# Moving tiles in SBUF so that no 256-column precise product of a two-model chain has both operands at one offset mod 256

## The chip, the cores and the metric

The kernel runs on one core of a Trainium2 chip. The metric is the device time of one execution in microseconds (us). The chip's TensorE (PE) does the matrix products, VectorE (DVE) and ScalarE (ACT) the elementwise work, GpSimd (POOL) a little of it, and SyncE (SP) issues most of the DMA.

## The reference

Two small transformers are chained: `first_block` gives x, `second_block` goes on with it. All arithmetic is float32, with 256 tokens and a width of 1024. The second model is what most of the time goes to:

```python
def second_block(x, positions, norm1_g, w_in, ..., w_up, w_down, final_g):
    for l in range(DEPTH):                      # 2 layers
        h = rmsnorm(x, norm1_g[l])
        z = h @ w_in[l]                         # 4 mixers' inputs and 4*1024 gate columns
        o_mla = mla_mixer(...); o_nsa = nsa_mixer(...)
        o_fox = fox_mixer(...); o_dsa = dsa_mixer(...)
        branches = jnp.stack([o_mla, o_nsa, o_fox, o_dsa], axis=2)
        lifted = jnp.einsum('bsnc,ncd->bsnd', branches, w_branch[l])
        gates = jax.nn.sigmoid(z_gate.reshape(B, S, N_BRANCH, D_MODEL))
        x = x + jnp.sum(gates * lifted, axis=2) @ w_out[l]
        h2 = rmsnorm(x, norm2_g[l])
        x = x + jnp.square(jax.nn.relu(h2 @ w_up[l])) @ w_down[l]   # 1024 -> 4096 -> 1024
    return rmsnorm(x, final_g)
```

`first_block` has two layers too: an even mixer (attention and pooling) and an odd mixer (gating and convolution), each followed by a mixture of experts with 16 experts, two for each token.

## The kernel before, in words

**Precise products.** TensorE multiplies in float32r, and one product of that is not precise enough. So `split` (L139 to L141) makes two tiles of each operand: ACT copies the value to a float32r tile (hi), DVE subtracts that from the value (lo). `mm3` (L167 to L170) then issues three products for one: hi by hi, hi by lo, lo by hi. Each has a stationary tile of 128x128 weights (`whi` or `wlo`), loaded by a LDWEIGHTS that the profile shows as PEld, and a moving tile of 128 partitions x 256 tokens of the activations. Such a product is called a 256-column product below, and a run of them over one half of a weight chunk a stream: 8 weight tiles, 24 products. `token_linear` (L201 to L203) has it the other way round: activations stand, 512 columns of weights move.

**Staging.** A chunk of weights is a 1 MB DMA into a slot of `ring` or `ring_b` (`chunk`, L132 on). `half` (L146 on) splits each half of it into `whi` and `wlo` of a staging pool, two buffers each, and turns to the next pool of the list `stages` for the next half. That list is `[stage]` in the first model, `[stage, stage_b]` in the second model, and `[stage, stage_b, ml]` in its feed-forward, where the pool `ml` is appended (L1638). So neighbouring streams read their weights from different pools.

**Pools.** Pools are laid out one behind the other in SBUF: `const`, `ring`, `stage`, then for the first model `c1` and `ring_b`, or for the second `wk`, `stage_b`, and behind them `at0`/`at1` (attention) or `ml0`/`ml1` (feed-forward). A change of a small tile in `const` shifts everything behind it. A tile's offset mod 256 below is its byte address within a partition modulo 256, as the built program has it; each 128-column weight tile takes 512 bytes and each 256-column moving tile 1024, so all products of a stream have the same two offsets. Before the change these are:

| stream (moving tile) | its offset | weights from: their offset |
|---|---|---|
| gates and other products with the normed x (`act`) | 0 | stage 0, stage_b 64 |
| branch lift `lf` and feed-forward up `fm` (`oT`) | 0 | stage 0, stage_b 64, ml 192 |
| output `fm` of the mixed branches (`mx`) | 64 | stage 0, stage_b 64 |
| feed-forward down `d` (`hid`) | 64 | stage 0, stage_b 64, ml 192 |
| mixers' `ah`/`al` of the first model | 0 | stage 0 |
| odd mixer's `mix` | 32 | stage 0 |

The **difference** of a stream is its weights' offset less its moving tile's, mod 256. It is 0 for 3175 pairs of neighbours among the program's 256-column products, 64 for 1650, 128 for 526, 192 for 1175, others for 656.

**Order of the work.** In attention `fill` (L1221 on) puts gate streams between the steps of the mixers, so that TensorE has work while softmax and top-k run on the other engines; the order is fixed in the program. The feed-forward of a layer (`up` at L1642, `down` at L1653) alternates up and down: 16 chunks each, each of two streams. The compressed attention makes `dv` (a doubled copy of the values, by POOL, L1411), transposes it on TensorE (`vct`, L1412), copies that on ACT (`vcT`, L1414), adds positions on POOL (`cblk`, L1426) and multiplies it with weights on TensorE (`cmp`, L1433 for keys, L1436 for values).

## Time and profile before

| | |
|---|---|
| runs | 1494.27, 1494.14, 1490.57 us; median 1494.14 us |
| profiled execution, own time | 1494.22 us |
| its span (first to last instruction) | 1492.5 us |
| mean granted TensorE clock | 0.985 of full speed |
| PE busy | 1453.1 us, 97% |
| DVE, ACT busy | 57%, 44% |
| DMA | 324.85 MB, mean 218 GB/s |

The span is one execution on the chip. An engine's share tells how much of the span it had an instruction running; matmuls overlap, so the busy time of a group of them (its count by its mean duration) is more than the time it takes, and the time that one product costs is the distance from its start to the next one's start.

### The profile page before, as it was taken

How to read it: one execution, taken by the hardware profiler on the slowest of the kernel's cores; microseconds unless marked ns; L12 is line 12 of the kernel's file. 1: busy time of each engine (PE TensorE's matmuls, PEld its weight loads, DVE VectorE, ACT ScalarE, POOL GpSimd, SP SyncE). 2: the span in 40 equal slices, each digit the busy share in tenths (PEclk: the TensorE clock that was granted, in tenths of full speed). 3: DMA queues.
4: the chain of work that ended last, by engine and by line, in shares of the span. 5: the costliest groups of instructions: out<-in, count | busy, mean ns of one | idle time of the engine just before them, and what ended most of it. 6: DMA issues, size and time to landing. Idle time of an engine off the chain costs nothing.

```text
span 1492.5 us, 25477 instructions
## 1 busy us (share of the span) xinstructions
PE 1453.1 (97%) x10370; PEld 1168.0 (78%) x10372; DVE 851.7 (57%) x1666; ACT 654.1 (44%) x1108; POOL 27.3 (2%) x63
## 2 busy tenths in 40 slices
PE   8999899989999998999999999999999999999998
PEld 3756644446985443798789999999898799999998
DVE  2765452126637222758776765556759767755554
ACT  2544311124433111565664554444565654644443
POOL 0000000000000000010000000000100000000000
PEclk9999999999999999999999999999999999999999
DMA  9964799949484986644125555553443234555540
GB/s 394 400 283 171 296 372 366 398 167 374 173 335 191 404 360 238 211 158 171 58 90 193 191 205 183 185 197 143 155 167 144 69 131 170 188 208 198 177 162 29
DMA packets 47006, 324.85 MB, mean 218 GB/s; under 512 B 5601, under 2 KB 5985, under 8 KB 8481
## 3 DMA queue, kind: packets, MB, share of 16 engines
q1 hardware_dynamic: 45360, 320.12, 56.3%
q8 instruction: 86, 1.41, 0.4%
q10 hardware_dynamic: 1296, 1.55, 0.3%
q0 software_dynamic: 224, 1.46, 0.3%
q14 instruction: 40, 0.32, 0.1%
HBM read 322.06 MB, written 1.05 MB: 216 GB/s over the span
## 4 chain that ended last, share of the span: by engine, by line
PE 57%; DVE 2%; ACT 1%; issue 0%; DVEq 0%; ACTq 0%
PE fm L169 10%; PE fm L170 10%; PE fm L168 10%; PE d L169 4%; PE d L168 4%; PE d L170 4%; PE sp L1504 1%; PE tm L201 1%; PE tm L202 1%; PE tm L203 1%; PE lf L169 1%; PE lf L170 1%; PE lf L168 1%; PE po L1493 1%; PE ptp L1487 1%; DVE wlo L141 1%
## 5 line engine op out<-in xcount | busy, mean ns | idle before, releaser
L141 DVE TENSOR_TENSOR wlo<-w,whi 128x1024 fp32r<-128x1024 f32 (+1 forms) x314 | 378.4, 1208 | 254.1 <-ACT whi L140 252.9
L140 ACT CAST whi<-w 128x1024 fp32r<-128x1024 f32 (+1 forms) x314 | 324.3, 1035 | 388.2 <-PE fm L169 234.7
L168 PE MATMUL fm<-acth,whi 128*128 128x256 f32 x592 | 169.4, 286 | 0.0
L169 PE MATMUL fm<-actl,whi 128*128 128x256 f32 x592 | 168.2, 284 | 0.0
L170 PE MATMUL fm<-acth,wlo 128*128 128x256 f32 x592 | 167.9, 284 | 0.0
L170 PE MATMUL d<-hidh,wlo 128*128 128x256 f32 x512 | 144.1, 282 | 0.0
L169 PE MATMUL d<-hidl,whi 128*128 128x256 f32 x512 | 144.0, 281 | 0.0
L168 PE MATMUL d<-hidh,whi 128*128 128x256 f32 x512 | 143.9, 281 | 0.0
L169 PE MATMUL fm<-oTl,whi 128*128 128x256 f32 x512 | 143.6, 281 | 0.0
L170 PE MATMUL fm<-oTh,wlo 128*128 128x256 f32 x512 | 143.3, 280 | 0.0
L168 PE MATMUL fm<-oTh,whi 128*128 128x256 f32 x512 | 143.1, 280 | 0.0
L169 PEld LDWEIGHTS fm<-actl,whi 128*128 128x128 f32 x592 | 112.5, 190 | 2.3 <-issue 2.3
L168 PEld LDWEIGHTS fm<-acth,whi 128*128 128x128 f32 x592 | 113.1, 191 | 1.0 <-issue 0.8
L170 PEld LDWEIGHTS fm<-acth,wlo 128*128 128x128 f32 x592 | 112.4, 190 | 1.3 <-issue 1.0
L169 PEld LDWEIGHTS fm<-oTl,whi 128*128 128x128 f32 x512 | 96.8, 189 | 0.4 <-DVE oTl L1118 0.4
L169 PEld LDWEIGHTS d<-hidl,whi 128*128 128x128 f32 x512 | 96.7, 189 | 0.4 <-DVE hidl L141 0.4
L168 PEld LDWEIGHTS fm<-oTh,whi 128*128 128x128 f32 x512 | 96.9, 190 | 0.0
L168 PEld LDWEIGHTS d<-hidh,whi 128*128 128x128 f32 x512 | 96.8, 189 | 0.1
L170 PEld LDWEIGHTS d<-hidh,wlo 128*128 128x128 f32 x512 | 96.8, 189 | 0.1
L170 PEld LDWEIGHTS fm<-oTh,wlo 128*128 128x128 f32 x512 | 96.8, 189 | 0.0
L600 PE MATMUL yp<-w,ht 128*64 128x512 f32 (+1 forms) x272 | 71.8, 622 | 6.6 <-PEq L791 3.2
L566 PE MATMUL gu<-w,ug 128*64 128x512 f32 x256 | 62.2, 598 | 0.0
(537 smaller groups left out, 2875.1 us busy)
## 6 DMA issues: line engine op xcount, KB each, us to landing
w<-gu SPq DMA_DIRECT2D x64, 1024.0 KB, 8.7
w<-mod SPq DMA_DIRECT2D x48, 1024.0 KB, 10.7
w<-dn SPq DMA_DIRECT2D x32, 1024.0 KB, 10.0
w<-gw SPq DMA_DIRECT2D x32, 1024.0 KB, 4.8
w<-up SPq DMA_DIRECT2D x32, 1024.0 KB, 4.7
w<-dw SPq DMA_DIRECT2D x32, 1024.0 KB, 4.7
w<-tm SPq DMA_DIRECT2D x12, 1024.0 KB, 4.9
w<-oin SPq DMA_DIRECT2D x8, 1024.0 KB, 8.8
```

The costliest lines, as they stand in the source:

```text
L140: A.copy(hi, src)
L141: V.tensor_sub(lo, src, hi.bitcast(F32))
L168: T.matmul(out, ws[0], xs[0], start=first, stop=False, skip_group_check=skip)
L169: T.matmul(out, ws[0], xs[1], start=False, stop=False, skip_group_check=skip)
L170: T.matmul(out, ws[1], xs[0], start=False, stop=last, skip_group_check=skip)
L201: T.matmul(ps, at[0], ww[0], start=first, stop=False, skip_group_check=True)
L202: T.matmul(ps, at[1], ww[0], start=False, stop=False, skip_group_check=True)
L203: T.matmul(ps, at[0], ww[1], start=False, stop=k == NK - 1, skip_group_check=True)
L566: T.matmul(gu[each * e:each * e + each, :], x_[:, 4 * h + k, s0 + CAP * e:s0 + CAP * e + each], w[e][:, 512 * k:512 * k + 512], start=(h = ...
L600: T.matmul(yp[each * e:each * e + each, :], ht[:, 128 * k + each * e:128 * k + each * e + each], wd[e][:, 1024 * k + 512 * q:1024 * k + 51 ...
L1487: T.transpose(tp[:, 128 * c:128 * c + 128], prs[g][:, 128 * c:128 * c + 128], ident)
L1493: T.matmul(po[64 * g:64 * g + 64, 0:S], vals(g, 0), prs[g][:, 0:S], start=first, stop=False, tile_position=(0, 64 * g), skip_group_check=True)
```

## The change: what it does, and the diff

The diff has three kinds of edits. A new function `apart` puts a tile of n floats at the beginning of a pool, which a memset on DVE fills once: 16 floats in `c1` and in `wk`, 48 in `at0`, `at1`, `ml0` and `ml1`. The gap within `ml` grows from 32 to 48 floats. And tiles are made smaller or shared: `epst` 8 floats instead of 16, one `g2` for both layers, `vss` in an existing tile, and `m8` (the eight maxima of top-k) and `dv` with one buffer instead of two.

`epst` and `g2` take 64 bytes from `const`, so that `ring` and `stage` begin at 192 instead of 0 mod 256; the 16 floats of `c1` and `wk` put back what lies behind them. The 48 floats move what lies in `at` and in `ml` ahead of the gap by 192.

```diff
+        def apart(pool, n):
+
+            V.memset(pool.tile([128, n], F32, name=f"gap{n}", tag=f"gap{n}"), 0.0)
...
         ring_b = b1.enter_context(tc.tile_pool(name="ring_b", bufs=7))
+        apart(c1, 16)
...
-        epst = const.tile([128, 16], F32, name="epst")[:, 0:1]
+        epst = const.tile([128, 8], F32, name="epst")[:, 0:1]
...
-            g2 = const.tile([128, NK], F32, name=f"g2_{layer}")
+            g2 = const.tile([128, NK], F32, name="g2", tag="g2")
...
-            ss = wk.tile([128, 8], F32, name="vss")
+            ss = wk.tile([128, S], F32, name="vss", tag="dg")[:, 0:8]
...
         wk = es.enter_context(tc.tile_pool(name="b2", bufs=1))
+        E["apart"](wk, 16)
...
             at = ph.enter_context(tc.tile_pool(name=f"at{l}", bufs=1))
+            E["apart"](at, 48)
...
-                    m8 = at.tile([128, 8], F32, name="m8", tag="m8", bufs=2)
+                    m8 = at.tile([128, 8], F32, name="m8", tag="m8")
...
-                dv = at.tile([128, 2, 64], F32, name="dv", tag="dv", bufs=2)
+                dv = at.tile([128, 2, 64], F32, name="dv", tag="dv")
...
             ml = ph.enter_context(tc.tile_pool(name=f"ml{l}", bufs=1))
+            E["apart"](ml, 48)
...
-                    V.memset(ml.tile([128, 32], F32, name="gap", tag="gap"), 0.0)
+                    V.memset(ml.tile([128, 48], F32, name="gap", tag="gap"), 0.0)
```

Offsets mod 256 in the program built from it: `ring` and `stage` 192, `stage_b` 64, `ml`'s weights 192; `act`, `oT`, `ah`/`al`, `mx`, `hid`, `mix` all 0. So a stream's difference is now that of its pool alone: 192 from `stage` and from `ml`, 64 from `stage_b`. In pairs of neighbours: 0 for 204 (in the experts' scatter, where no split weights take part), 64 for 2420, 192 for 4074, others for 466.

The products are the same, in the same number. Two places are in another order. With one buffer of `dv`, its second copy on POOL must follow the first transpose, and TensorE's second transpose stands behind half of the keys' `cmp` products. TensorE in layer 1 before:

```order
L1412 MATMUL vct<-cst,dv 128x128 [waits Activation_49]
L1412 MATMUL vct<-cst,dv 128x128
L1433 MATMUL cmp<-cblk,w 64x16 [waits DMAHW3_49,Activation_49,Pool_49]
L1433 MATMUL cmp<-cblk,w 64x16 x7
L1433 MATMUL cmp<-cblk,w 64x16 [waits Pool_49]
L1433 MATMUL cmp<-cblk,w 64x16 x7
L1504 MATMUL sp<-fk,fq 128x128 x2
```

and now:

```order
L1419 MATMUL vct<-cst,dv 128x128 [waits Activation_49]
L1440 MATMUL cmp<-cblk,w 64x16 [waits DMAHW3_49,Activation_49,Pool_49]
L1440 MATMUL cmp<-cblk,w 64x16 x7
L1419 MATMUL vct<-cst,dv 128x128 [waits Pool_49]
L1440 MATMUL cmp<-cblk,w 64x16 x8
L1511 MATMUL sp<-fk,fq 128x128 x2
```

`vct` is the tile of transposed values, `cmp` the compressed keys, `sp` the next scores. The second transpose waits for POOL (its copy of `dv`) and stands behind 8 of the 16 `cmp` products; on POOL the second copy went behind the four sums of `cblk` for the keys and waits for TensorE. The second layer has the same.

The memsets of the gaps come where their pools first open. DVE at the end of the first model and the start of the second before (`ygl` and `y` are the last experts' outputs, `xT` the residual sum, `actl` the lo part of the second model's first activations):

```order
L606 SCALAR_TENSOR_TENSOR ygl<-yp,cws,ygh 128x512 [waits Activation_49]
L425 SCALAR_TENSOR_TENSOR xT<-y_4537,g_1_4541,xT 128x256 [waits PE_49]
L141 TENSOR_TENSOR wlo<-w,whi 128x1024 [waits DMAHW4_49,DMAHW3_49,DMAHW5_49,DMAHW2_49,DMAHW6_49,DMAHW1_49,DMAHW7_49,DMAHW0_49,Activation_49]
L606 SCALAR_TENSOR_TENSOR ygl<-yp,cws,ygh 128x512 [waits Activation_49]
L1118 SCALAR_TENSOR_TENSOR actl<-xT,pf,acth 128x256 [waits Activation_49]
L425 SCALAR_TENSOR_TENSOR xT<-y_4537,g_1_4541,xT 128x256
L141 TENSOR_TENSOR wlo<-w,whi 128x1024 [waits Activation_49]
L1118 SCALAR_TENSOR_TENSOR actl<-xT,pf,acth 128x256 [waits Activation_49]
L425 SCALAR_TENSOR_TENSOR xT<-y_4538,g_1_4541,xT 128x256 [waits PE_49]
L425 SCALAR_TENSOR_TENSOR xT<-y_4538,g_1_4541,xT 128x256
```

and now:

```order
L80 MEMSET gap_6265 128x16 [waits DMAHW3_49,DMAHW2_49,DMAHW4_49,DMAHW1_49,DMAHW5_49,DMAHW0_49,DMAHW6_49,DVE_49,DMAHW7_49,PE_49,Activation_49]
L611 SCALAR_TENSOR_TENSOR ygl<-yp,cws,ygh 128x512 [waits Activation_49]
L430 SCALAR_TENSOR_TENSOR xT<-y_4539,g_4543,xT 128x256 [waits PE_49]
L146 TENSOR_TENSOR wlo<-w,whi 128x1024 [waits DMAHW2_49,Activation_49]
L611 SCALAR_TENSOR_TENSOR ygl<-yp,cws,ygh 128x512 [waits Activation_49]
L1124 SCALAR_TENSOR_TENSOR actl<-xT,pf,acth 128x256 [waits Activation_49]
L430 SCALAR_TENSOR_TENSOR xT<-y_4539,g_4543,xT 128x256
L146 TENSOR_TENSOR wlo<-w,whi 128x1024 [waits Activation_49]
L80 MEMSET gap_6279 128x48 [waits DMASW1_49,DMASW2_49,DMASW0_49,DMASW3_49,SP_sequencer_49,DMASW4_49,DVE_sequencer_49,DMASW5_49,PE_sequencer_49,DMASW6_49,Activation_sequencer_49,DMASW7_49,Pool_sequencer_49,DMAHW6_49,DVE_49,PE_49]
L1124 SCALAR_TENSOR_TENSOR actl<-xT,pf,acth 128x256 [waits Activation_49]
L430 SCALAR_TENSOR_TENSOR xT<-y_4540,g_4543,xT 128x256 x2
```

The gap of `wk` stands ahead of the residual sums and waits for the first model's last readers of that memory, the gap of `at0` stands between the second model's first `actl` tiles and waits for TensorE's last product of the experts; the two sums behind it no longer have that wait of their own. On DVE, too, each MAX of top-k now follows the MATCH_REPLACE that reads the one `m8`. The gap of `at1` stands the same way at the start of the second layer. The order on SP is the same.

## Rows read from the trace of the kernel before

**Rows 1.** The page, part 1: busy time, share, instructions of each engine.

```profile
PE 1453.1 (97%) x10370; PEld 1168.0 (78%) x10372; DVE 851.7 (57%) x1666; ACT 654.1 (44%) x1108; POOL 27.3 (2%) x63
```

**Rows 2.** Windows: stretch; busy us by engine; PEclk; DMA share; GB/s.

```profile
470.00:605.00 135.00, 128.97 (x657) 60.41 (x656) 48.01 (x135) 29.99 (x50) 1.23 (x6) 0.99 0.84 335
...
700.00:770.00 70.00, 69.51 (x522) 55.25 (x520) 50.35 (x153) 44.89 (x133) 0.00 (x0) 0.99 0.26 92
...
870.00:1055.00 185.00, 185.00 (x1517) 182.47 (x1516) 107.22 (x121) 88.04 (x108) 0.96 (x5) 1.00 0.50 177
```

**Rows 3.** Instructions by line, PE: group xcount | busy us, mean ns.

```profile
L168 PE MATMUL fm<-acth,whi 128*128 128x256 f32 x592 | 169.4, 286 | 0.0
...
L168 PE MATMUL d<-hidh,whi 128*128 128x256 f32 x512 | 143.9, 281 | 0.0
...
L168 PE MATMUL fm<-oTh,whi 128*128 128x256 f32 x512 | 143.1, 280 | 0.0
...
L168 PE MATMUL fm<-ah,whi 128*128 128x256 f32 x192 | 54.9, 286 | 0.3 <-DVE mod L406 0.3
```

**Rows 4.** Timeline, PE, feed-forward: start us, duration us of each stream's first product.

```profile
910.50 0.28 PE L168 MATMUL fm<-oTh,whi 128*128 128x256 f32 x1
...
927.61 0.28 PE L168 MATMUL d<-hidh,whi 128*128 128x256 f32 x1
...
930.46 0.28 PE L168 MATMUL d<-hidh,whi 128*128 128x256 f32 x1
...
933.29 0.29 PE L168 MATMUL fm<-oTh,whi 128*128 128x256 f32 x1
...
936.02 0.28 PE L168 MATMUL fm<-oTh,whi 128*128 128x256 f32 x1
...
938.74 0.28 PE L168 MATMUL d<-hidh,whi 128*128 128x256 f32 x1
...
941.46 0.28 PE L168 MATMUL d<-hidh,whi 128*128 128x256 f32 x1
...
944.34 0.28 PE L168 MATMUL fm<-oTh,whi 128*128 128x256 f32 x1
```

**Rows 5.** Timeline, PE, gate streams in attention: first products of three streams.

```profile
783.25 0.28 PE L168 MATMUL fm<-acth,whi 128*128 128x256 f32 x1
...
786.07 0.28 PE L168 MATMUL fm<-acth,whi 128*128 128x256 f32 x1
...
788.95 0.28 PE L168 MATMUL fm<-acth,whi 128*128 128x256 f32 x1
```

**Rows 6.** Timeline, PE, odd mixer: the first and last of 313 products.

```profile
374.03 0.28 PE L170 MATMUL fm<-ah,wlo 128*128 128x256 f32 x1
...
411.47 0.28 PE L170 MATMUL fm<-ah,wlo 128*128 128x256 f32 x1
```

**Rows 7.** Timeline, PE, ACT and POOL around the value transposes of layer 1.

```profile
694.71 0.38 PE L1412 MATMUL vct<-cst,dv 128*128 128x128 f32 x2
...
695.02 2.04 PE L1433 MATMUL cmp<-cblk,w 128*64 128x16 f32 x32
...
696.18 1.79 POOL L1426 TENSOR_TENSOR cblk<-vcT,pe 64x120 f32<-64x120 f32 x4 [34.44 <-ACT vcT L1414]
...
698.55 1.25 PE L1436 MATMUL cmp<-w,cblk 128*16 128x64 f32 x10
```

**Rows 8.** Timeline, DVE, ACT, PE where the second model begins.

```profile
599.55 0.87 DVE L425 SCALAR_TENSOR_TENSOR xT<-y,g,xT 128x256 f32<-128x256 f32 x2
...
600.86 0.91 ACT L1117 ACTIVATE acth<-xT,pf 128x256 fp32r<-128x256 f32 x2
...
601.41 0.73 PE L201 MATMUL tm<-whi,acth 128*128 128x512 f32 x2 [0.52 <-ACT acth L1117]
```

**Rows 9.** DMA issues: KB of one, median us from issue to landing.

```profile
pw<-pool_w SPq DMA_DIRECT2D x1, 256.0 KB, 2.6
sgw<-sg_w ACTq DMA_DIRECT2D x1, 256.0 KB, 4.2
```

## The prediction, made before the changed kernel ran

> **What bounds the kernel now.** I read the page's shares first, then windows by stage, then the groups of products by line, and last the timeline of TensorE alone, where the time of a product is the distance between starts. The shares say that PE is busy for 97% of the span [rows 1]; the reader is to see that no other engine comes near. The windows say where it has no slack at all: in the feed-forward of layer 1 PE is busy for 185.00 us of 185.00, with DMA at half its share and the clock at 1.00; in attention for 69.51 of 70 [rows 2]. So almost all of the second model is as long as its products, and what a product costs decides. The groups by line say which they are: 592, 512, 512 and 192 products on each of the three lines of `mm3` [rows 3].
>
> Their mean durations differ a little, 286 against 280 ns, though they are the same work. The timeline tells what this goes with. In the feed-forward each stream of 24 products has one pair of offsets, and in the order of rows 4 the differences are: from 927.61 `hid` with ml, 128; from 930.46 `hid` with stage, 192; from 933.29 `oT` with stage_b, 64; from 936.02 `oT` with ml, 192; from 938.74 `hid` with stage, 192; from 941.46 `hid` with stage_b, 0. A stream's length by 24 gives the spacing [rows 4]:
> - difference 128: 2.85 us, 118.8 ns
> - 192 at 930.46: 2.83 us, 117.9 ns
> - 64, 192 and 192 after it: 2.73, 2.72 and 2.72 us, 113.3 to 113.8 ns
> - 0: 2.88 us, 120.0 ns
>
> The gate streams in attention alternate: at 783.25 with stage_b, difference 64, 2.82 us or 117.5 ns; at 786.07 with stage, difference 0, 2.88 us or 120.0 ns [rows 5]. In the odd mixer, where all weights come from stage at difference 0, 312 spacings take 37.44 us, 120.0 ns each [rows 6]. So a difference of 0 always costs 120.0, and others have two levels, about 117.7 and 113.4. A stream behind one at 0 or 128 has the slower one here; once a stream is at the faster one, the next non-zero stream stays there.
>
> **What the change does to the products.** No stream keeps a difference of 0 or 128; each has 64 or 192. What they cost then no row shows for long. The nearest stretch is the one from 930.46 to 941.46, four streams with neither 0 nor 128: 11.00 us for 96 products, 114.6 ns [rows 4]. It is bounded below by 113.4, every stream at the faster level, and above by 117.7, every stream at the slower one. I take 115.5, half of the products at either level: nearer to the stretch than to the upper end, but with returns to the slower level allowed for, since in that stretch the moving tile also changes between `hid` at 64 and `oT` at 0, which it no longer does.
> - **Feed-forward.** 512 up and 512 down products on each of three lines [rows 3], 3072. A cycle of twelve streams from 910.50 to 944.34 takes 33.84 us for 288 products, 117.5 ns [rows 4]. 3072 x (117.5 - 115.5) = 6.1 us gained.
> - **Gates and the rest with `act`.** 592 x 3 = 1776 [rows 3]. Half at 120.0, half at 117.5 [rows 5], mean 118.8. 1776 x 3.3 = 5.9 us.
> - **Branch lift.** 8 chunks of 16 weight tiles, three products each, 384 by the code, with the offsets of the gates: 384 x 3.3 = 1.3 us. The products of the mixed branches are as many, with one class at 0 and one at 192, as in the feed-forward: 384 x 2.0 = 0.8 us.
> - **Odd mixer and the even one's output.** 192 x 3 = 576 [rows 3], from 120.0 [rows 6]. They have one pool, so a run of one difference; I take the slower level, which a stream has that starts behind something else: 576 x 2.3 = 1.3 us.
> - The `mix` products had a difference other than 0 before, and the 512-column ones of `token_linear` move other tiles; for both I count nothing.
>
> Sum: 6.1 + 5.9 + 1.3 + 0.8 + 1.3 = 15.4 us gained.
>
> **What it costs.** The transposes. Before, both run at 694.71, `cmp` follows at 695.02 for 2.04 us, POOL starts `cblk` for the values at 696.18 once `vcT` is there, and PE waits 0.63 us at 698.55 for POOL's last sum [rows 7]. Now the second transpose is behind half of `cmp`, 1.0 us later. ACT's copy, then POOL's sums and the values' `cmp` are late by what isn't covered, with nothing on PE's queue able to pass. Between 0 and 1.0 us a layer. I take 0.3: POOL started only at 696.18, 1.1 us after the transposes ended, so ACT's copy between them was late for another reason and covers most of it. For two layers 0.6. POOL's second copy itself waits for the first transpose and is short beside the 1.0 us.
>
> The memset of `at0`'s gap stands, with its chain of semaphores, ahead of the residual sums that start at 599.55 and take 0.87, until 600.42; ACT begins the activations from them at 600.86, and PE waits 0.52 us for those at 601.41 [rows 8]. 0.44 us of DVE's delay are covered there, the rest is PE's. The wait itself takes the place of the one that the two sums behind it had for the same products. Between 0 and 0.6 us; I take 0.2. The gap of `at1` waits for PE where a sum waited for PE before; the others are in idle stretches of DVE, which is busy for 107.22 us of 185 [rows 2]. MAX behind MATCH_REPLACE costs nothing, as each already reads what the other wrote.
>
> Cover. In attention, products shortened beside a chain on DVE and ACT give back only where PE would not wait instead. PE idles 0.49 us of 70 [rows 2], so most of the gain stays; I take off 0.7 us, 200 gate products of either layer at half of 3.3 ns.
>
> 15.4 - 0.6 - 0.2 - 0.7 = 13.9 us. From the profiled execution's 1494.22 us, 0.08 over the median of the runs, this gives 1480.3, so **1480 us**.
>
> **Rivals.**
> - **The faster level holds throughout.** Nothing in rows 4 ends it but a difference of 0, and none is left. At 113.4: feed-forward 12.6, gates 9.6, lift 2.1, mixed branches 1.6, mixers 3.8, together 29.7; less 1.5 of costs, 28.2: 1466 us. Against it: streams at 64 and 192 sit at the slower level too, for all their 24 products [rows 4, 5], with no drift back.
> - **The difference does little.** Every stream settles at 117.7, the level of those that start behind another kind of work. Then the feed-forward loses 0.6 us, gates gain 2.0, lift 0.4, the mixed branches nothing and mixers 1.3; less 1.5 it is 1.6 us: 1492.6. It includes that the offsets only go along with something else, such as which engine writes at the time; against that, `hid` with stage is fast and `hid` with stage_b is slow within 3 us [rows 4]. The Trainium skill, page "TensorE: Matmul & The Clock Gate", section "Part 2: What happens when you issue a matmul", speaks for no effect: PE has two independent read ports into SBUF, and "Loading the next tile's weights doesn't steal SBUF read bandwidth from the running matmul", by which no offset could matter and the time would be 1494.2 plus the 0.8 us of costs, 1495. The trace does not agree: 2.88 against 2.72 us for the same 24 products [rows 4].
> - **Slower: the ring's slots are no longer aligned.** Four of the slots that 1 MB weight loads go to now begin at 192 mod 256. `sgw`, which began at 32 mod 256, took 4.2 us for 256 KB, `pw` at offset 0 took 2.6 [rows 9], a factor of 1.6, with other traffic beside both. The experts of the second layer load at a DMA share of 0.84 [rows 2]; with 4 of 13 turns of the list `rings` there through `ring`, a factor f makes that 0.84 x (1 + 4/13 x (f - 1)). It decides from f = 1.6, where the share is 1.0. At f = 2 it is 1.10: 135 us become 148, and if the first layer's experts lose half as much, 20 us are lost against 14 won, 1500 us. Against it: the ratio of rows 9 holds one transfer each, issued from different queues at different times.
>
> **Chances.** The middle forecast (1471 to 1488) 0.53, the faster level throughout 0.26, little effect 0.16, slower through loads 0.05. The range has to reach to the faster level and leaves out the last two: 1465 to 1490, 0.79. A measurement of this kernel tells some 0.3% or 4.5 us from no change: faster is below 1489.7, slower above 1498.6. Faster: 0.53 + 0.26 + 0.02 of the little effect = 0.81. Same: 0.14. Slower: 0.05.
>
> **What would show it.** In the changed kernel's timeline of the feed-forward, a cycle of twelve streams should take 33.3 us instead of 33.84 (32.7 if the faster level holds, 33.9 if the slower), with no stream of 2.88 or 2.85. In attention no gate stream should take 2.88. In the odd mixer 312 spacings should take 36.7 us. The PE wait ahead of the values' `cmp` should grow from 0.63 to about 0.9, and the wait at the second model's start from 0.52 to about 0.7. The windows of the experts (470 to 605) should keep their length; if they grow with DMA near 1.00, the loads are slower. The prediction is wrong if streams without a difference of 0 still take 2.88 us, or if DVE or a load becomes what PE waits for in the feed-forward.

## The result, and the profile after

The changed kernel takes 1474.95 us, the median of four runs from 1471.55 to 1478.32, against 1494.12 before; the ratio is 0.9882 with a 95% interval from 0.9859 to 0.9906. The prediction was 1480 us within 1465 to 1490. Run again beside two experiments it took 1476.28 us, ratio 0.9891 [0.9874, 0.9909]. The kernel before took a median of 1491.25 to 1491.94 us beside the experiments, 2 to 3 us less than beside this first result, so by medians the gain is 15.6 to 19.2 us. The profiled execution is the longest of the first four, 1478.32 us with a span of 1476.5, so the two traces differ by 16.0 us of span, less than the medians do.

The page of the changed kernel, parts 1 and 5 (two groups as in rows 3, now on L173 and L175):

```profile
PE 1435.1 (97%) x10370; PEld 1148.0 (78%) x10372; DVE 852.4 (58%) x1672; ACT 654.3 (44%) x1108; POOL 27.3 (2%) x63
...
L173 PE MATMUL fm<-acth,whi 128*128 128x256 f32 x592 | 166.7, 282 | 0.0
...
L175 PE MATMUL fm<-acth,wlo 128*128 128x256 f32 x592 | 165.0, 279 | 0.7 <-DVE wlo L146 0.7
```

PE is busy for 97% of the span as before [rows 1] and does the same 10370 instructions in 18 us less. The gates' mean duration fell from 286 to 282 ns [rows 3]. What a product costs is again read from starts. TensorE's timeline in the feed-forward of layer 1, first products of every fourth stream and of a cycle's end:

```profile
884.40 0.28 PE L173 MATMUL fm<-oTh,whi 128*128 128x256 f32 x1
...
895.71 0.28 PE L173 MATMUL fm<-oTh,whi 128*128 128x256 f32 x1
...
906.59 0.28 PE L173 MATMUL fm<-oTh,whi 128*128 128x256 f32 x1
...
939.23 0.28 PE L173 MATMUL fm<-oTh,whi 128*128 128x256 f32 x1
```

From 884.40 to 895.71 four streams (96 products) take 11.31 us, 117.8 ns a product: the slower level. The four from 895.71 to 906.59 take 10.88, 113.3 ns, and from 906.59 to 939.23 the cycle of twelve streams takes 32.64 us where before it took 33.84 [rows 4]. No stream falls back from there to the layer's last product, at 1031.6. In attention, the gate streams from stage_b and from stage (rows 5 before):

```profile
777.07 0.28 PE L173 MATMUL fm<-acth,whi 128*128 128x256 f32 x1
...
779.79 0.28 PE L173 MATMUL fm<-acth,whi 128*128 128x256 f32 x1
...
782.51 0.28 PE L173 MATMUL fm<-acth,whi 128*128 128x256 f32 x1
```

Both take 2.72 us, 113.3 ns. In the odd mixer, with one pool, the first and last of 319 products (rows 6 before):

```profile
373.20 0.28 PE L175 MATMUL fm<-ah,wlo 128*128 128x256 f32 x1
...
410.65 0.28 PE L175 MATMUL fm<-ah,wlo 128*128 128x256 f32 x1
```

37.45 us for 318 spacings, 117.8 ns: the slower level all through. Where the time went, by the first products of each stage in the two traces (us; less is faster):

| stretch | before | after | difference |
|---|---|---|---|
| first model up to the second's first product | 596.17 | 597.88 | +1.7 |
| layer 1, input products | 39.94 | 40.16 | +0.2 |
| layer 1, attention to the feed-forward | 221.59 | 216.60 | -5.0 |
| layer 1, feed-forward to the next layer | 182.83 | 177.07 | -5.8 |
| layer 2, input products | 37.25 | 37.41 | +0.2 |
| layer 2, attention to the feed-forward | 220.46 | 218.42 | -2.0 |
| layer 2, feed-forward to its last product | 182.70 | 177.06 | -5.6 |
| the rest | 11.53 | 11.95 | +0.4 |

Three windows of the changed kernel, in the experts, in the feed-forward of layer 1 and in the attention of layer 2 (columns as in rows 2):

```profile
470.00:605.00 135.00, 128.67 (x652) 59.82 (x651) 46.63 (x135) 28.28 (x47) 1.22 (x6) 0.99 0.83 334
...
895.70:1030.00 134.30, 134.30 (x1187) 134.30 (x1186) 74.84 (x76) 62.73 (x72) 0.00 (x0) 1.00 0.53 191
...
1131.00:1156.80 25.80, 25.41 (x209) 21.50 (x207) 21.87 (x63) 12.90 (x35) 0.04 (x1) 0.93 0.42 163
```

The experts' stretch has the DMA share and the busy time that it had [rows 2]. The stretch from 1131.0 to 1156.8, which lies behind the values' `cmp` of layer 2, is some 1.2 us longer than the same stretch before: its granted clock is 0.93, so TensorE was at 1.2 GHz for part of it. The same two stretches of the kernel before, layer 1 and layer 2:

```profile
698.50:724.30 25.80, 25.41 (x210) 21.47 (x209) 21.28 (x63) 12.87 (x34) 0.00 (x0) 0.95 0.44 162
...
1140.20:1164.80 24.60, 24.09 (x209) 20.11 (x209) 21.32 (x63) 12.95 (x35) 0.00 (x0) 1.00 0.46 173
```

There the lower clock stood in layer 1 and none in layer 2. So of the 3 us that layer 2 gains less in attention than layer 1, some 2.2 are the clock's, which took about 1.1 us from layer 1 before and takes it from layer 2 now.

### The profile page after: what moved, and what is told of

It reads as the page before. It is cut to its first block, busy times and chain, and to the rows that moved or that the text cites. A ratio compares the mean times of both kernels' runs of the same rounds, so it can differ in the third digit from the quotient of the medians.

```text
span 1476.5 us, 25487 instructions
## 1 busy us (share of the span) xinstructions
PE 1435.1 (97%) x10370; PEld 1148.0 (78%) x10372; DVE 852.4 (58%) x1672; ACT 654.3 (44%) x1108; POOL 27.3 (2%) x63
## 4 chain that ended last, share of the span: by engine, by line
PE 55%; DVE 3%; ACT 1%; issue 0%; DVEq 0%; ACTq 0%
PE fm L174 9%; PE fm L173 9%; PE fm L175 9%; PE d L174 4%; PE d L173 4%; PE d L175 4%; PE tm L206 1%; PE tm L208 1%; PE tm L207 1%; PE sp L1511 1%; DVE wlo L146 1%; PE po L1500 1%; PE ptp L1494 1%; PE lf L175 1%; PE lf L174 1%; PE lf L173 1%
## 5 line engine op out<-in xcount | busy, mean ns | idle before, releaser
L173 PE MATMUL fm<-acth,whi 128*128 128x256 f32 x592 | 166.7, 282 | 0.0
L175 PE MATMUL fm<-acth,wlo 128*128 128x256 f32 x592 | 165.0, 279 | 0.7 <-DVE wlo L146 0.7
L175 PE MATMUL d<-hidh,wlo 128*128 128x256 f32 x512 | 142.0, 277 | 0.0
L173 PE MATMUL d<-hidh,whi 128*128 128x256 f32 x512 | 141.8, 277 | 0.0
L175 PE MATMUL fm<-oTh,wlo 128*128 128x256 f32 x512 | 141.5, 277 | 0.0
L173 PE MATMUL fm<-oTh,whi 128*128 128x256 f32 x512 | 141.2, 277 | 0.0
L175 PEld LDWEIGHTS fm<-acth,wlo 128*128 128x128 f32 x592 | 111.2, 188 | 1.8 <-DVE wlo L146 1.1
L173 PEld LDWEIGHTS fm<-acth,whi 128*128 128x128 f32 x592 | 111.4, 188 | 0.9 <-issue 0.8
L173 PEld LDWEIGHTS d<-hidh,whi 128*128 128x128 f32 x512 | 96.1, 188 | 0.1
L175 PEld LDWEIGHTS d<-hidh,wlo 128*128 128x128 f32 x512 | 96.1, 188 | 0.1
L175 PEld LDWEIGHTS fm<-oTh,wlo 128*128 128x128 f32 x512 | 96.1, 188 | 0.0
L173 PEld LDWEIGHTS fm<-oTh,whi 128*128 128x128 f32 x512 | 96.0, 188 | 0.0
L387 PE MATMUL mps<-w,cpad 128*32 128x512 f32 x384 | 57.7, 626 | 5.0 <-DMA w<-mod 4.8
```

The lines of the kernel that those rows point to most:

```text
L173: T.matmul(out, ws[0], xs[0], start=first, stop=False, skip_group_check=skip)
L175: T.matmul(out, ws[1], xs[0], start=False, stop=last, skip_group_check=skip)
L387: T.matmul(self.ps[32 * k:32 * k + 32, :], cpad[:, 4 * h + k, 32 - 2 * at:64 - 2 * at], w[:, k, :], start=(at == 0 and h == 0), stop=(h == 1),
```

## The experiments

All kernels but e5 to e7 start from the changed one; the difference is weights' offset less moving tile's, mod 256. Where the first model adds to the noise, times are also given from the second model's first product to the span's end: 896.3 us in the kernel before, 878.7 and 878.1 in the two profiled executions of the changed one. Each edit moves addresses by pads, and apart from e7, e10 and e11 TensorE's order stays that of the kernel that it starts from.

**e1, every stream at 0.**

```diff
-        epst = const.tile([128, 8], F32, name="epst")[:, 0:1]
+        epst = const.tile([128, 24], F32, name="epst")[:, 0:1]
-        apart(c1, 16)
-        E["apart"](wk, 16)
+        E["apart"](stage_b, 24)
-            E["apart"](at, 48)
-            E["apart"](ml, 48)
-                if cj == 0:
-                    V.memset(ml.tile([128, 48], F32, name="gap", tag="gap"), 0.0)
```

> The changed kernel with its pads moved so that stage, stage_b and ml all begin where the moving tiles do: every stream of split weights has difference 0, TensorE's order is that of the changed kernel. If a difference of 0 is what costs, every stream takes 120.0 ns a product: a feed-forward cycle of twelve streams 34.56 us (changed kernel about 32.8), the odd mixer's 312 spacings 37.4, and the whole about 30 us over the changed kernel, 1505 us, 11 over before. If the gain came from something else in the edit (smaller tiles, the order of the transposes, another place of the moving tiles), it stays at about 1475.

Measured: 1513.12 us, ratio to before 1.0145 [1.0121, 1.0169]. First products of twelve streams' beginning and end in the feed-forward of layer 1 (down streams):

```profile
909.16 0.28 PE L172 MATMUL d<-hidh,whi 128*128 128x256 f32 x1
...
943.72 0.28 PE L172 MATMUL d<-hidh,whi 128*128 128x256 f32 x1
```

34.56 us, 120.0 ns for each of 288 products, as foreseen. The feed-forward gives 17.9 us of the 35.5 between this span (1512.0) and the changed kernel's; that it is 38 over the changed kernel and not 30 is for the most part one stretch of layer 2, behind `cmp`:

```profile
1148.50:1180.20 31.70, 31.31 (x209) 25.61 (x209) 20.34 (x61) 12.97 (x34) 0.35 (x1) 0.75 0.35 131
```

It takes 31.7 us at a clock of 0.75, 5.8 us more than in the changed kernel. Another 1.4 us in each layer lie between the first transpose and the values' `cmp` (5.18 us instead of 3.80), for a reason that e7 shows. So 0 is the costly difference, in the place and the size forecast, and the order of the transposes and the clock add to it.

**e2 and e3, one difference for all.** e2 has 192 in every stream, e3 64 in every stream of the second model.

```diff
 e2
         stage_b = es.enter_context(tc.tile_pool(name="stage_b", bufs=2))
+        E["apart"](stage_b, 16)
-            E["apart"](at, 48)
+            E["apart"](at, 16)
-            E["apart"](ml, 48)
+            E["apart"](ml, 16)
 e3
-        E["apart"](wk, 16)
+        E["apart"](wk, 48)
-                    V.memset(ml.tile([128, 48], F32, name="gap", tag="gap"), 0.0)
+                    V.memset(ml.tile([128, 80], F32, name="gap", tag="gap"), 0.0)
```

> The changed kernel with stage_b at 192 as well: every stream has difference 192, none alternates with 64. If only the difference of 0 costs and any other is fast, about 1475 as the changed kernel, the feed-forward cycle 32.8 us. If a stream keeps the level that the one before it had and 192 starts at the slower level (as most streams do in the changed kernel that start at 192 behind a wait), the feed-forward cycle takes 33.9 us, and 5600 products at 117.7 instead of 114.1 cost 20 us: 1493 to 1495.

> The changed kernel with all moving tiles of the second model at 128 and ml's weights back at 192: every stream of the second model has difference 64. If any difference but 0 is fast: about 1475. If the level is kept and only the border from 192 to 64 leads to the faster one: streams that start at 64 behind a wait were fast in 8 of 20 cases in the changed kernel, so between 1475 and 1495, some 1484, and the feed-forward cycle is either 32.7 or 33.9 us throughout, by how it starts.

Measured: e2 1492.73 us, ratio 1.0023 [1.0000, 1.0047], all of the gain gone; e3 1475.63 us, ratio 0.9901 [0.9876, 0.9925]. The cycle of twelve streams in e2:

```profile
906.78 0.28 PE L173 MATMUL fm<-oTh,whi 128*128 128x256 f32 x1
...
940.70 0.28 PE L173 MATMUL fm<-oTh,whi 128*128 128x256 f32 x1
```

and in e3:

```profile
903.04 0.28 PE L173 MATMUL fm<-oTh,whi 128*128 128x256 f32 x1
...
935.68 0.28 PE L173 MATMUL fm<-oTh,whi 128*128 128x256 f32 x1
```

33.92 us at 192, 117.8 ns, and 32.64 at 64, 113.3 ns. It is not enough that the difference isn't 0, and the first reading above, that any difference but 0 is as good, is wrong. But 192 does not exclude the faster level. In e2's mixed branches of layer 1 five streams run at it:

```profile
840.39 0.28 PE L173 MATMUL fm<-mxh,whi 128*128 128x256 f32 x1
...
853.99 0.28 PE L173 MATMUL fm<-oTh,whi 128*128 128x256 f32 x1
```

13.60 us for 120 products, 113.3 ns, at the same offsets as the streams at 117.8. And in e3's attention many streams are slow: from the first lift to the mixed branches layer 1 takes 109.0 us, between 108.2 in the changed kernel and 110.5 before. In both kernels an uninterrupted run of streams keeps the level that it starts with, at each of the 194 borders between streams of the second model. What differs is the start behind other work: at 192 it was slow 37 times of 38, at 64 fast 23 times of 38. In the changed kernel the runs start slow 27 times of 38, but a slow one turned fast at 11 of 16 borders from 192 to 64, and none turned slow at any of the 167 borders behind a fast one. So the mixture of the two, in which a stream at 64 mostly leads to the faster level and those at 192 stay on it, is as good as 64 alone.

**e4, the odd mixer at 64.**

```diff
         with tc.tile_pool(name="l1", bufs=1) as wk:
+            apart(wk, 32)
```

> The changed kernel with 128 bytes ahead of the odd mixer's tiles: its 384 products from x and 192 from mix have difference 64 instead of 192, all else as in the changed kernel. If 64 can start at the faster level, 312 spacings take 35.4 us instead of 36.7 and the whole is 1 to 2 us under the changed kernel, about 1473; if one pool with one difference stays at the slower level, 36.7 us and no change, 1475.

Measured: 1473.15 us, ratio 0.988 [0.986, 0.990]. The same first and last of 319 products as above:

```profile
372.26 0.28 PE L175 MATMUL fm<-ah,wlo 128*128 128x256 f32 x1
...
408.31 0.28 PE L175 MATMUL fm<-ah,wlo 128*128 128x256 f32 x1
```

36.05 us for 318 spacings, 113.4 ns instead of 117.8, 1.4 us in this stretch. By the medians e4 gains 1.8 us, which the intervals don't set apart; by the trace the 1.4 us are there.

**e5 and e6, the two parts alone**, each on the kernel before. Both define `apart`. e5 has the pads of `c1` and `wk`, the smaller `epst` and one `g2`, so that ring and stage stand at 192; e6 has the pads of `ml`.

```diff
 e5
-        epst = const.tile([128, 16], F32, name="epst")[:, 0:1]
+        epst = const.tile([128, 8], F32, name="epst")[:, 0:1]
+        apart(c1, 16)
-            g2 = const.tile([128, NK], F32, name=f"g2_{layer}")
+            g2 = const.tile([128, NK], F32, name="g2", tag="g2")
+        E["apart"](wk, 16)
 e6
+            E["apart"](ml, 48)
-                    V.memset(ml.tile([128, 32], F32, name="gap", tag="gap"), 0.0)
+                    V.memset(ml.tile([128, 48], F32, name="gap", tag="gap"), 0.0)
```

> The kernel before with one part of the change: ring and stage at 192 (smaller epst, one g2, the pads of c1 and wk), the feed-forward's hid and gap left. Gates and lift have differences 192 and 64, the up streams 192, 64, 192, the down streams 128, 0, 128. If streams of 0 and 128 cost themselves and also send the streams behind them to the slower level, the gates gain as in the change (1776 products at 114.4 instead of 118.5 and the lift: 8 to 9 us) and the feed-forward's cycle stays at about 33.8 us: 1483. If the gain comes with the ring and stage alone, the cycle is 32.8 us and the whole 1475.

> The kernel before with the other part alone: the pad of 48 and the gap of 48 floats in the feed-forward, so that hid is at 0; stage stays at 0. Up and down streams alike have differences 0, 64, 192 in turn; gates as before. If every stream of 0 sends the next ones back to the slower level, the cycle gains little: a third at 120.0, the rest between 113.4 and 117.7, 33.4 to 34.1 us against 33.84, the whole 1486 to 1495. If the two parts add up (feed-forward 11.6 us of the change's gain by this part), 1481.

Measured: e5 1486.81 us, ratio 0.9965 [0.9953, 0.9976]; e6 1493.86, ratio 1.0023 [1.0008, 1.0037]. The cycle in e5:

```profile
906.67 0.28 PE L173 MATMUL fm<-oTh,whi 128*128 128x256 f32 x1
...
940.46 0.28 PE L173 MATMUL fm<-oTh,whi 128*128 128x256 f32 x1
```

33.79 us, as before the change (33.84), while attention from the first lift to the mixed branches takes 108.3 us in layer 1 as in the full change. In e6 (layer 1, twelve streams):

```profile
908.65 0.28 PE L172 MATMUL fm<-oTh,whi 128*128 128x256 f32 x1
...
942.76 0.28 PE L172 MATMUL fm<-oTh,whi 128*128 128x256 f32 x1
```

34.11 us, a little more than before. The two parts do not add up: -4.4 and +2.6 us by the medians against -15.6 to -19.2 together; from the second model's first product on, -8.3 and +1.7 against -17.6. The reading that a stream of 0 or 128 sends the next ones back to the slower level holds for 0 in e6, where 62 of 64 streams at 64 behind one at 0 are slow, but not for 128: in e5 the streams at 64 behind one at 128 are fast, ten times of ten, as here:

```profile
929.28 0.28 PE L173 MATMUL fm<-oTh,whi 128*128 128x256 f32 x1
...
932.02 0.28 PE L173 MATMUL fm<-oTh,whi 128*128 128x256 f32 x1
```

2.74 us for 24 products. A cycle of e5 has three such streams at 113.3 ns, three at 192 that take 117.8, four at 128 and two at 0, which cost their own price. The feed-forward's 11.4 us came only where no stream of 0 or 128 was left in it.

**e7, the change's order without its offsets.** On the kernel before:

```diff
-                    m8 = at.tile([128, 8], F32, name="m8", tag="m8", bufs=2)
+                    m8 = at.tile([128, 8], F32, name="m8", tag="m8")
-                dv = at.tile([128, 2, 64], F32, name="dv", tag="dv", bufs=2)
+                dv = at.tile([128, 2, 64], F32, name="dv", tag="dv")
```

> The kernel before with m8 and dv at one buffer and nothing else: the change's order of the transposes and of MAX without its offsets. The prediction's price is 0.6 us for both layers; by the changed kernel's trace it is nearer to 0.3 (the values' cmp 0.04 us earlier after vct in one layer, 0.25 later in the other). Neither is clear of noise: the whole 1492, and the distance from vct to the values' cmp says which: 3.8 in both layers, or 4.2.

Measured: 1500.03 us, ratio 1.0061 [1.0043, 1.0080]: a cost of 8.8 us by the medians that neither reading foresaw. The runs' mean granted clock is 0.979 to 0.988, that of the kernel before beside it 0.984 to 0.991, and the longest runs have the lowest clocks (1503.9 us at 0.979). The profiled execution is the shortest one (1492.3), with a first model 5.0 us shorter than in the kernel before, which has the same code there. From the second model's first product on it takes 899.4 us instead of 896.3, 3.1 us more. 2.5 of them lie between the first transpose and the first lift of layer 1, 0.5 in the same stretch of layer 2. In layer 1 the values' `cmp` starts 5.31 us after the first transpose instead of 3.84:

```profile
690.22 1.40 POOL L1411 COPY dv<-zv 128x128 f32<-128x128 f32 x1 [33.29 <-PE vct L1412]
...
690.25 1.22 DVE L141 TENSOR_TENSOR wlo<-w,whi 128x1024 fp32r<-128x1024 f32 x1
...
691.67 0.33 PE L1412 MATMUL vct<-cst,dv 128*128 128x128 f32 x1 [0.55 <-POOL dv L1411]
```

POOL's second copy of `dv`, which this order puts behind the first transpose, took 1.40 us and ended 0.15 us after DVE's subtraction for `wlo`, and PE stood still for 0.55 us until it was done. In the changed kernel the same copy takes 0.29 us. In e1 it began 0.01 to 0.04 us behind the subtraction in both layers, took 1.33 and 1.35 and ended again 0.15 us after it, with 0.49 and 0.51 us of waiting on PE. In the other profiled executions with this order it began 0.03 to 0.32 us ahead and took 0.29 to 0.30, though in some the subtraction began while it ran. In e7 it began 0.03 us ahead in both layers, and took 1.40 in layer 1 and 0.29 in layer 2, where the distance is 3.80. So the order is cheap where the copy gets ahead of the subtraction, and dear where it ends only after it. Around and behind it the clock was lower too:

```profile
688.00:696.00 8.00, 7.45 (x68) 5.97 (x67) 7.65 (x25) 2.43 (x4) 4.24 (x5) 0.82 0.63 203
```

How the 3.1 us divide between the wait and the clock, and whether the copy was late more often in the long runs, was not traced; their lower clocks are on record.

**e8 and e9, two other differences.** All three staging pools at 192, the second model's moving tiles at 96 and at 64:

```diff
-        E["apart"](wk, 16)
+        E["apart"](wk, 40)
         stage_b = es.enter_context(tc.tile_pool(name="stage_b", bufs=2))
+        V.memset(stage_b.tile([128, 8], F32, name="gapb", tag="gapb", bufs=1), 0.0)
-            E["apart"](at, 48)
+            E["apart"](at, 40)
-            E["apart"](ml, 48)
+            E["apart"](ml, 40)
-                    V.memset(ml.tile([128, 48], F32, name="gap", tag="gap"), 0.0)
+                    V.memset(ml.tile([128, 88], F32, name="gap", tag="gap"), 0.0)
```

This is e8; e9 has 32, 16, 32, 32 and 96 in these places.

> The changed kernel with the second model's moving tiles at 96 and all three staging pools at 192: every stream of the second model has difference 96, which neither kernel has. If the faster level belongs to everything but 0, 128 and a run of 192, the cycle takes 32.7 us; if it belongs to 64 (and to what follows it), 33.9 or an irregular 34.2 as at 128.

> The changed kernel with the second model's moving tiles at 64 and all three staging pools at 192: every stream of the second model has difference 128. In the kernel before the down streams of 128 took 118.6 ns a product with irregular steps, but each stood beside a stream of 0 or 64. If that is 128's own price, the feed-forward's cycle takes 34.2 us and the whole is 25 us over the changed kernel, 1498 to 1502; if it was the neighbours' doing, a run of 128 settles at a level of the others: 33.9 us and 1493, or 32.7 and 1475.

Measured: e8 1505.23 us in its one run, e9 1500.59 us, ratio 1.0047 [1.0033, 1.0061]. The cycle in e8:

```profile
909.63 0.28 PE L173 MATMUL fm<-oTh,whi 128*128 128x256 f32 x1
...
943.80 0.28 PE L173 MATMUL fm<-oTh,whi 128*128 128x256 f32 x1
```

and in e9:

```profile
910.63 0.28 PE L173 MATMUL fm<-oTh,whi 128*128 128x256 f32 x1
...
944.80 0.28 PE L173 MATMUL fm<-oTh,whi 128*128 128x256 f32 x1
```

34.17 us in both, 118.6 ns. In layer 2 e9's cycle is the same, but e8's is longer:

```profile
1336.29 0.28 PE L173 MATMUL fm<-oTh,whi 128*128 128x256 f32 x1
...
1370.85 0.28 PE L173 MATMUL fm<-oTh,whi 128*128 128x256 f32 x1
```

34.56 us, 120.0 ns, as at a difference of 0; in e8's attention some streams take 117.3. So 128 has a price of its own, near that of 0, also where nothing else stands beside it, and 96 has more than one. Some of e8's excess over e9 is this, and some the clock: its stretch behind `cmp` in layer 2 is 31.5 us long, as in e1. In e2, e3, e8 and e9 all weights of the second model stand at 192 and only the moving tiles differ, between e1 and e2 only the weights' place against the moving tiles at 0: the level goes with both places together.

**e10 and e11, the order of before with the better offsets.** Both start from e4. e11 puts the two copies of `dv` in one tile that exists already, so that the transposes stand together again; e10 also gives `m8` its second buffer, which leaves TensorE, POOL and SP with the order of the kernel before.

```diff
-            for b in range(2):
-                dv = at.tile([128, 2, 64], F32, name="dv", tag="dv")
+            dvs = wk.tile([128, 2, 2, 64], F32, name="dv", tag="dg")
+            for b in range(2):
+                dv = dvs[:, b]
 e10 only
-                    m8 = at.tile([128, 8], F32, name="m8", tag="m8")
+                    m8 = at.tile([128, 8], F32, name="m8", tag="m8", bufs=2)
```

> The offsets of e4 (odd mixer at difference 64), with two buffers of m8 and the two dv copies in one shared tile, so that TensorE, POOL and SP have the order of the kernel before. e7 showed the order of the change alone to cost 9 us over before in most of its runs, at a granted clock of 0.979 to 0.985 instead of 0.988. If that cost lies in the changed kernel too, this one is 3 to 9 us under it in the same call, 1464 to 1470, at a clock of 0.987 to 0.989. If it belongs to e7 only (to its offsets, or to that stretch of runs), 1473 as e4.

> The same, but m8 with one buffer: only the transposes go back to their old place. If the second transpose behind half of the cmp products is what lowers the clock, as e10; if the longer chain of MAX and MATCH_REPLACE (and the few gate products that it moves) is, 1473 as e4.

> The changed kernel once more, so that the two above are compared with it on the same chip: 1475 as first measured (1471.5 to 1478.3), clock 0.984 to 0.989.

Measured: e10 1470.77 us, ratio 0.9858 [0.9838, 0.9878]; e11 1471.20, ratio 0.9865 [0.9844, 0.9886]; the changed kernel beside them 1476.28, ratio 0.9891 [0.9874, 0.9909]. The stretch behind `cmp` of layer 2 in e10:

```profile
1125.00:1149.60 24.60, 24.02 (x210) 20.06 (x209) 21.42 (x64) 13.04 (x35) 0.00 (x0) 1.00 0.45 172
```

24.6 us at a clock of 1.00, and 24.8 in e11, against 25.9 at 0.93 in both profiled runs of the changed kernel and in e4. But e10 has the lower clock in layer 1 instead, e2 with the change's order has it there too, and e3 with that order in neither layer. One execution of each therefore doesn't tell whether the order sets it. e10 has the lowest median of all kernels here, 5.5 us under the changed one beside it, of which e4's edit is a part; the intervals of the two ratios still touch. By that median the first reading, a cost of the order in the changed kernel too, seems borne out, but the traces put the gain elsewhere. The second model's first product in e10, and then in the changed kernel beside it:

```profile
590.34 0.50 PE L206 MATMUL tm<-whi,acth 128*128 128x512 f32 x1 [0.48 <-ACT acth L1124]
```

```profile
596.95 0.50 PE L206 MATMUL tm<-whi,acth 128*128 128x512 f32 x1 [0.48 <-ACT acth L1123]
```

6.6 us lie ahead of it, 1.4 of them e4's edit, in a first model whose order is the same in both. From there on e10 takes 878.2 us, e11 876.9, e4 878.0 and the changed kernel 878.1. And first models with one code differ by up to 5.0: the kernel before, e6 and e7 reach this product at 596.17, 593.80 and 591.18. That the best version takes about 1471 us is measured; that the order of before is worth anything once the offsets are right is not shown.

## Why the prediction was right, point by point

The forecast was the middle case, by offsets that decide between levels, and the time fell between it and the rival of the faster level throughout, which would have given 1466. The mechanism is right, one of its terms was too small, and that the total is near is partly luck. The sum has 6.1 us for the feed-forward, 6.7 for attention and 1.1 for the first model with the memset; by the two traces these are 11.4, 7.0 and -1.7, with another -0.8 in the input products and at the end. The first model's loss is within what executions with one code differ by there, and it hid half of what the feed-forward gained beyond the forecast.

- **A difference of 0 costs 120.0 ns, always.** Held for whole streams, and shown by e1; in attention, pieces of 11 to 14 products at 0 took 118.4 to 118.7 in the kernel before. The other half of that reading, that a stream behind one at 0 has the slower level, has an exception in the same trace: mixed-branch streams at 192 behind one at 0, from 849.4 and 855.0, took 113.3.
- **The level without it, taken as 115.5 ns.** This is the term that was mis-sized. The feed-forward settled at 113.3 [rows 4 for the cycle before], so it gained 11.4 us and not 6.1; that is the rival's term of 12.6 less early streams of each layer, many of which still ran at 117.8. I had allowed for returns to the slower level and within an uninterrupted run there were none. But the rival's reason, that nothing but 0 ends the faster level, is only half of it: other work between two runs ends it as well, and what leads back is the border from 192 to 64. e2 has no 0 and no such border, and there almost every stream stays at the slower level. Neither case had that.
- **Gates, lift and mixed branches, 5.9 + 1.3 + 0.8 less the costs there of 1.3.** 6.7 us forecast, 7.0 measured in the two layers, though the 96 gate products that `gate_steps` issues itself (L1239) were not in the 1776. The streams gained more than foreseen, 120.0 and 117.5 to 113.3 where they run undisturbed [rows 5]. Against that stand a new wait of PE for DVE's lo tiles, 0.7 us in all (the row of L175 above, 0.0 before), which is the cover that I had taken off, and the clock in layer 2.
- **The mixers at the slower level.** Held: 117.8 ns where 117.7 was taken [rows 6]. The first model as a whole did not gain, though: it ends 1.7 us later. Kernels with the same code there differ by more, up to the second model's first product 596.17 us before, 593.80 in e6 and 591.18 in e7, so this isn't put down to a part of the change.
- **The transposes, 0.6 us of waits.** Too much here: 0.2 us for both layers. TensorE, ACT and POOL of the changed kernel in layer 1 (rows 7 before):

```profile
695.29 0.27 PE L1419 MATMUL vct<-cst,dv 128*128 128x128 f32 x1
...
695.49 1.10 PE L1440 MATMUL cmp<-cblk,w 128*64 128x16 f32 x16
...
695.70 0.29 POOL L1418 COPY dv<-zv 128x128 f32<-128x128 f32 x1 [32.72 <-PE vct L1419]
...
696.53 0.33 PE L1419 MATMUL vct<-cst,dv 128*128 128x128 f32 x1
...
696.90 0.37 ACT L1421 COPY vcT<-vct 128x256 f32<-128x256 f32 x1 [0.48 <-PE vct L1419]
...
699.09 1.12 PE L1443 MATMUL cmp<-w,cblk 128*16 128x64 f32 x17
```

The second transpose indeed stands behind half of `cmp`, 1.24 us after the first; POOL's copy takes 0.29 us and is done long before. The values' `cmp` at 699.09 is 3.80 us behind the first transpose, against 3.84 before: ACT's copy had been late anyway, so all of it is covered. In layer 2 the distance grows by 0.25 us. The wait of 0.63 us that the prediction read as PE's is that of its weight loads (PEld), in the kernel before and now:

```profile
698.55 1.09 PEld L1436 LDWEIGHTS cmp<-w,cblk 128*16 128x16 f32 x11 [0.63 <-POOL cblk L1426]
```

```profile
699.09 1.00 PEld L1443 LDWEIGHTS cmp<-w,cblk 128*16 128x16 f32 x18 [0.33 <-POOL cblk L1433]
```

PE itself had score products running up to there in both, and before they ran at a lowered clock, so the fall from 0.63 to 0.33 says nothing of the order; in layer 2 it is 0.33 in both kernels. The price that was missing is the one that e7 shows: POOL's copy is short only as long as it is ahead of DVE's subtraction.
- **The gaps' memsets, 0.2 us at the second model's start.** DVE and TensorE there (rows 8 before):

```profile
600.90 0.10 DVE L80 MEMSET gap<- 128x48 f32 x1
...
603.12 0.73 PE L206 MATMUL tm<-whi,acth 128*128 128x512 f32 x2 [0.52 <-ACT acth L1123]
```

The memset of `at0`'s gap takes 0.10 us, and PE's wait for the activations is 0.52 as before, where I expected 0.7: covered.
- **Loads into a ring at 192 mod 256.** The rival on the other side fell. The page's DMA issues of the changed kernel:

```profile
w<-gu SPq DMA_DIRECT2D x64, 1024.0 KB, 8.4
...
w<-gw SPq DMA_DIRECT2D x32, 1024.0 KB, 4.9
```

The experts' `gu`, of which only some go into `ring`, took 8.4 us, and before 8.7, at the DMA share that the experts had. The gates' `gw` all go into `ring`: 4.9 us, and before 4.8. So no factor near 1.6 goes with an offset of 192; what slowed the one transfer of rows 9 is not shown.
- **That the offsets don't matter** (two independent read ports, by the Trainium skill's page "TensorE: Matmul & The Clock Gate", section "Part 2: What happens when you issue a matmul"). e1 and e3 differ in offsets (and in where a pad's memset stands) and by 37 us, of which some 9 are the clock and the transposes; the feed-forward's cycle alone is 34.56 against 32.64 us. The measurement decides against the rule for this pair of streams.

## What to carry to other kernels

When a long run of equal products is all that an engine does, print the distance from start to start, by operand tile: two or three levels in it point to where the tiles lie, and a pad of some tens of bytes can move all of them. What one part of such an edit gains can be nothing while another part is missing, as the levels are kept from stream to stream, so the parts are tested together as well as alone. And an edit made only to find space (a buffer less) is part of the change: here, alone, it cost 9 us by the medians (e7), as a short copy came to stand where another engine's work can make it nearly five times as long, while the memsets of the pads cost nothing that could be seen. Before a median's few us are put down to an edit, it pays to see in the traces on which side of the edited code they lie.

## What the runs showed of the hardware that was not expected

- Float32r products of 256 columns with new weights each time, by the difference between weights and moving tile, mod 256, in the feed-forward: 113.3 ns at 64 (e3); 117.8 at 192 alone (e2); 118.6 at 128 (e9); 118.6 in one layer and 120.0 in the other at 96 (e8); 120.0 at 0 (e1). At 2.4 GHz 113.3 ns is 272 cycles and 120.0 is 288. 64 and 192 share two levels, 113.3 and 117.8, and a run of streams keeps the one that it starts with (e2, e3). No other difference was run in a whole feed-forward. The reason for it is not shown by a run, nor what decides the level at a start.
- Behind the products of 16 columns of `cmp` the granted clock fell in some layers and not in others: in the profiled executions of the kernel before, e2, e6, e7 and e10 in layer 1, of the changed kernel, e4 and e8 in layer 2, of e1 and e9 in both, of e3, e5 and e11 in neither. It took about 1.1 us in the changed kernel (25.9 us in layer 2 against 24.9 in layer 1) and some 7 in e1. Runs of one kernel differ by up to 1.1% (e2, 1489.87 us at a mean clock of 0.988 and 1505.84 at 0.938), more than most single terms of the sum. What decides it was not found: it followed each of the three late copies of `dv` (e1 in both layers, e7 in layer 1), but came without one too.
- A copy of 128x128 on POOL took 0.29 us where it began ahead of DVE's subtraction of two 128x1024 tiles, and 1.33 to 1.40 where it began behind it or, once, 0.03 us ahead; it then ended 0.15 us after the subtraction (e1, e7).
